# A decoder layer in split fp32: later slices of the up projection as 512-column products, and a new written order

## The chip, the cores and the metric

The kernel runs on one core of a Trainium2 chip. The time is the device time of one execution in microseconds; the median of several runs is given. The profile is of one further execution. TensorE multiplies, VectorE and ScalarE do elementwise work, GpSimd sets constants, and SyncE (SP) issues nearly all transfers.

## What is computed

One decoder layer on 256 tokens (S) of width 1024 (D), batch 1, with an adaptive norm whose shifts, scales and gates come from a conditioning vector c:

```python
mod = (c @ w_ada + b_ada)              # sh1, sc1, g1, sh2, sc2, g2
h = rmsnorm(x, norm1_g) * (1 + sc1) + sh1
z = h @ w_in                           # q, k, v, xr, gr
...                                    # attention (8 heads of 64), RG-LRU with a conv of width 4
x = x + g1 * (mix @ w_out)
h2 = rmsnorm(x, norm2_g) * (1 + sc2) + sh2
up = causal_dwconv(h2 @ w_up, ffn_conv_w, ffn_conv_b)     # width 3, 2 * 2816 columns
gate, val = split(up)
x = x + g2 * ((silu(gate) * val) @ w_down)
```

Everything is fp32 at the kernel's border.

## The kernel before

**Split products.** A weight block w is cast to a high part `wh` (`hi`, L158; L144 on ScalarE, or L150 on VectorE with a last argument 1), and the rest is `wl = w - wh` (`lo`, L172, VectorE). The activations are split the same way: for norm n and k block kt, `normed` (VectorE) makes x times scale times 1/rms, `h_hi` the high part with the shift added (ScalarE, or VectorE with argument 1), `h_lo` the rest (VectorE). The parts are two tiles `hh` and `hl` of 8 k blocks by 256 tokens. Each logical product is then three: `wh` with `hh`, `wh` with `hl`, `wl` with `hh`, summed in PSUM.

**Stages.** (1) Beginning: loads; `x_sq`, `x_sum`, `norm_s`, `norm_r`, `norm_mm` make 1/rms for norm 1; `m1_mm`, `m1_row`, `m1_col`, `m1_add` make scale and shift of the first k blocks from two loads of w_ada ("g1" 0 and 1) by a vector product, a copy of the row, a turn into a column and an add; `warm_up(n)` issues n filler products on a constant; `sp` are 18 tiny VectorE steps on the RG-LRU's decay. (2) `lin`: the input projection over 8 k blocks, with `x`, `g`, `q` as 256-column products and `k` as 512-column ones; `ada` computes further columns of mod with reductions on VectorE. (3) `v`, convolution, gates, the scan, attention. (4) `wo`: output projection. (5) norm 2: `res`, `res_sq`, `res_add`, `res_sum` (one block each), four vector products `g1_mm(6)` to `g1_mm(9)` with `g1_row`, `g1_col`, `g1_add` for its scale, `norm_s`, `norm_r`, `norm_mm`, then `normed`, `h_hi`, `h_lo` block by block. (6) The channel part: 22 slices f of 128 gate and 128 value columns. `up(f, kt)` does six products for one k block into one bank (four banks in turn). `gated_a` (ScalarE) reads the bank with the last tap's weight and the bias, `gated_d` (VectorE) adds two shifted taps, both out of PSUM; then `gated_s` (SiLU), `gated_m`, `gated_h`, `gated_l`, and `down(f, m)` with three products for each of 8 output blocks.

**Order.** Every engine works in the order in which the calls are written. From the first call to slice 3 of `up` they are written out one by one (some 640 calls); from slice 4 on a loop issues `up(f)`, the `gated` steps of f - 1 with the weight splits of f + 1 between them, and `down(f - 2)`. In the passes f = 7, 9, 11 and 13 two reductions `ada("g2", ...)` stand in it as well.

**Loads.** `order` is the list of weight loads, 1 MB each, sent on SP's queue into six buffers, the next whenever one comes free (`used`). The vector c in 128 copies (`cb`, 512 KB) is sent between them; only `ada` needs it. The split weights have three buffers.

Of the kernel before, what the change touches and what calls it, by code (L numbers as in the profile page):

```python
# [49 lines left out]
NSPLIT = 3  # L50

# [17 lines left out]
def hybrid_layer(ctx: ExitStack, tc: tile.TileContext, x_d, c_d, pk_d, bd_d, ada1_d, lin_d, v_d,  # L69
# [36 lines left out]
    order += [("g1", 2), ("g1", 3), ("wo", 0), ("g1", 4), ("g1", 5), ("wo", 1)]  # L106
# [647 lines left out]
    def gated_a(f):  # L754
        cv = get(T, ("cv", f), m4)
        for s in range(2):
            i = 2 * f + s
            nc.scalar.activation(cv[:, s, :], pair(B["up", f])[:, s, :], AF.Identity, scale=col(O_FW + 88 + i),  # L758
                                 bias=col(O_FB + i))

    def gated_d(f, s):
        cv = T["cv", f]
        i = 2 * f + s
        for j in (1, 0):
            d = 2 - j
            nc.vector.scalar_tensor_tensor(cv[:, s, d:], pair(B["up", f])[:, s, :S - d], col(O_FW + 44 * j + i),  # L766
# [33 lines left out]
    kept.enter_context(tc.manual_schedule())  # L800
    warm_up(9)
    x_sq(0)
    x_sq(1)
    consts()
    c_cols()
    x_add(0, 1)
    x_sq(2)
    x_add(0, 2)
    x_sq(3)
# [7 lines left out]
    sp_act()  # L817
    warm_up(2)
    sp(0)
    warm_up(4)  # L820
    m1_mm(0, 1, 4)
    norm_mm("n1")
    m1_row(0, 0)
    m1_row(0, 1)
    m1_col(0, 0)
    norm_c()
    m1_col(0, 1)
    m1_add(0, 0)
    normed(0, 0)
    hi("lin", 0, 0)  # L830
    m1_add(0, 1)
    sp(1)
    h_hi(0, 0, 1)
    sp(2)
    hi("lin", 0, 1)
    h_lo(0, 0)
    warm_up(2)
    lin(0, "x", 0)
    lin(0, "x", 1)
    lin(0, "g", 0)  # L840
    lin(0, "g", 1)
    m1_mm(1, 0, 7)
    lo("lin", 0, 1)
    m1_row(1, 0)
    sp(3)
    lo("lin", 0, 0)
    lin(0, "q", 1)
    m1_col(1, 0)
    lin(0, "q", 0)
    m1_mm(1, 1, 7)  # L850
    m1_row(1, 1)
    hi("lin", 1, 0)
# [707 lines left out]
```

## Time and profile before

| | |
|---|---|
| runs | 332.77 us median of 3 (332.19 to 333.26) |
| the profiled execution | 332.59 us, its span 330.8 us |
| granted TensorE clock over the span | 0.991 |
| TensorE busy | 320.2 us (97%) |
| VectorE busy | 263.0 us (79%) |
| ScalarE busy | 194.5 us (59%) |
| read from memory | 76.43 MB, 234 GB/s over the span |

The span runs from the first to the last instruction; some 1.8 us of the time lie around it. Products are pipelined: one is shown with its whole way through the array, so distances between starts tell the rate, and a busy TensorE can still stand between two instructions. The granted clock is the share of full speed that the chip gives TensorE.

### The profile page before, as it was taken

To read this page: it belongs to the slowest core of one execution; us is meant where nothing else is said; L and a number is where in the kernel's file an instruction comes from. 1 tells how busy PE (TensorE), PEld (TensorE's weight loads), DVE (VectorE), ACT (ScalarE), POOL (GpSimd) and SP (SyncE) were. 2 spreads that over 40 slices of the span, in tenths; PEclk is the share of its full clock that TensorE was granted. 3 is DMA by queue.
4 is the path that set the end of the run, shared out by engine and by line. 5 is a ranking of instruction groups with operands and counts; after the bars stand their busy time and mean duration, and the time that the engine had idled before them with its cause. 6 is when DMAs were issued, how large, how long until landed. Compare 5 with 4: busy or idle time off the path is not lost.

```text
span 330.8 us, 6467 instructions
## 1 busy us (share of the span) xinstructions
PE 320.2 (97%) x2608; PEld 302.6 (91%) x2608; DVE 263.0 (79%) x507; ACT 194.5 (59%) x328; POOL 4.6 (1%) x22
## 2 busy tenths in 40 slices
PE   7899999999999999899999999999999999999994
PEld 7789999767599996899999999999999999999994
DVE  2469999899999998968696788888888677685654
ACT  5635458999988245865566455464646464655520
POOL 5000000000000000000000000000000000000000
PEclk9999999999999999799999999999999999999998
DMA  7999999939355998836566557575849463300003
GB/s 224 337 405 408 410 408 422 411 136 385 131 162 206 345 407 316 348 129 254 167 223 248 174 214 264 206 293 183 323 146 364 135 242 133 129 0 2 3 0 127
DMA packets 18013, 77.89 MB, mean 235 GB/s; under 512 B 1600, under 2 KB 6336, under 8 KB 10944
## 3 DMA queue, kind: packets, MB, share of 16 engines
q1 hardware_dynamic: 17840, 77.34, 62.6%
q8 instruction: 20, 0.33, 0.4%
q10 hardware_dynamic: 144, 0.15, 0.2%
q14 instruction: 9, 0.07, 0.1%
HBM read 76.43 MB, written 1.05 MB: 234 GB/s over the span
## 4 chain that ended last, share of the span: by engine, by line
PE 69%; DVE 16%; ACT 6%; issue 3%; SPq 2%; DMA 2%; DVEq 0%; ACTq 0%
PE bank L65 68%; DVE wl L172 4%; DVE w L365 4%; DMA w<-in_dram 2%; DVE m L423 2%; ACT wh L144 1%; SPq L132 1%; DVE m L766 1%; PE bank L676 1%; DVE ht L381 1%; ACT p L670 1%; DVE m L794 1%; DVE m L458 1%; DVE wh L150 1%; SPq L181 1%
## 5 line engine op out<-in xcount | busy, mean ns | idle before, releaser
L172 DVE TENSOR_TENSOR wl<-w,wh 128x1024 fp32r<-128x1024 f32 x94 | 113.2, 1220 | 19.8 <-ACT wh L144 19.1
L144 ACT CAST wh<-w 128x1024 fp32r<-128x1024 f32 x90 | 92.1, 1043 | 43.6 <-PE bank L65 34.9
L65 PE MATMUL bank<-hh__1575,wh 128*128 128x256 f32 x352 | 71.6, 285 | 1.1 <-ACT hh__1575 L148 1.1
L65 PE MATMUL bank<-hl__1576,wh 128*128 128x256 f32 x352 | 71.7, 286 | 0.0
L65 PE MATMUL bank<-hh__1575,wl 128*128 128x256 f32 x352 | 71.6, 285 | 0.0
L65 PEld LDWEIGHTS bank<-hh__1575,wh 128*128 128x128 f32 x352 | 55.3, 193 | 1.3 <-ACT hh__1575 L148 1.3
L65 PEld LDWEIGHTS bank<-hl__1576,wh 128*128 128x128 f32 x352 | 55.6, 194 | 0.2 <-DVE hl__1576 L392 0.2
L65 PEld LDWEIGHTS bank<-hh__1575,wl 128*128 128x128 f32 x352 | 55.4, 194 | 0.2 <-DVE wl L172 0.2
L766 DVE SCALAR_TENSOR_TENSOR m<-bank,pk,m 128x255 f32<-128x255 f32 x88 | 40.4, 479 | 19.0 <-ACT m L758 17.4
L65 PE MATMUL bank<-pl,wh 128*128 128x256 f32 x176 | 49.9, 284 | 0.4 <-DVE pl L782 0.4
L65 PE MATMUL bank<-ph,wh 128*128 128x256 f32 x176 | 49.9, 284 | 0.0
L65 PE MATMUL bank<-ph,wl 128*128 128x256 f32 x176 | 49.8, 283 | 0.0
L65 PEld LDWEIGHTS bank<-pl,wh 128*128 128x128 f32 x176 | 33.8, 192 | 0.6 <-DVE pl L782 0.6
L65 PEld LDWEIGHTS bank<-ph,wh 128*128 128x128 f32 x176 | 33.8, 192 | 0.1
L65 PEld LDWEIGHTS bank<-ph,wl 128*128 128x128 f32 x176 | 33.8, 192 | 0.0
L758 ACT ACTIVATE m<-bank,pk 128x256 f32<-128x256 f32 x44 | 22.4, 558 | 18.9 <-PE bank L65 18.9
L365 DVE CUSTOM_DVE_ANT_0 w<-w,cb 128x1024 f32<-128x1024 f32 x22 | 26.3, 1218 | 0.0
L770 ACT ACTIVATE m<-m 128x256 f32<-128x256 f32 x22 | 9.2, 417 | 26.8 <-DVE m L766 26.8
L65 PE MATMUL bank<-hl_mix__1178,wh 128*128 128x256 f32 x64 | 18.3, 286 | 0.2 <-DVE hl_mix__1178 L505 0.2
L65 PE MATMUL bank<-hh_mix__1177,wh 128*128 128x256 f32 x64 | 18.4, 288 | 0.0
L65 PE MATMUL bank<-hh_mix__1177,wl 128*128 128x256 f32 x64 | 18.1, 283 | 0.0
L65 PE MATMUL bank<-hh__245,wh 128*128 128x256 f32 x96 | 14.8, 283 | 1.0 <-DVE lt L345 1.0
(176 smaller groups left out, 429.5 us busy)
## 6 DMA issues: line engine op xcount, KB each, us to landing
w<-in_dram SPq DMA_DIRECT2D x55, 1024.0 KB, 5.1
w<-in_dram SPq DMA_DIRECT2D x32, 512.0 KB, 10.1
xT<-in_dram SPq DMA_DIRECT2D x4, 256.0 KB, 4.5
cb<-in_dram SPq DMA_DIRECT2D x1, 512.0 KB, 9.7
out_dram<-m SPq DMA_DIRECT2D x4, 128.0 KB, 2.5
out_dram<-m SPq DMA_DIRECT2D x2, 256.0 KB, 2.8
m<-in_dram SPq DMA_DIRECT2D x1, 256.0 KB, 9.5
pk<-in_dram ACTq DMA_DIRECT2D x1, 145.0 KB, 4.0
```

The costliest lines, as they stand in the source:

```text
L65: self.nc.tensor.matmul(out, lhsT, rhs, start=left == self.n, stop=left == 1, skip_group_check=True)
L132: (q or nc.sync).dma_start(raw[key][:, c:c + n], srcs[key[0]][key[1]][:, c:c + n])
L144: nc.scalar.copy(out, in_)
L150: nc.vector.tensor_copy(out, in_)
L172: (nc.vector if e else nc.gpsimd).tensor_sub(l[:, c], raw[key][:, c], h.bitcast(F32)[:, c])
L181: nc.sync.dma_start(xT[:, 2 * i:2 * i + 2, :], x_d[:, 2 * i:2 * i + 2, :])
L365: nc.vector.tensor_tensor_reduce(v[:, a, :], v[:, a, :], cb, scale=scale, scalar=0.0, op0=ALU.mult, op1=ALU.add, accum_out=mod[:, j, kt:kt ...
L381: nc.vector.scalar_tensor_tensor(T["ht", n, kt], xT[:, kt, :], mod[:, (SC1, SC2)[n], kt:kt + 1], rep, op0=ALU.mult, op1=ALU.mult)
L423: nc.vector.scalar_tensor_tensor(xc[:, t, s:], pair(B["x", t // 2])[:, t % 2, :S - s], col(O_CW + 4 * j + t), xc[:, t, s:], op0=ALU.mult, ...
L758: nc.scalar.activation(cv[:, s, :], pair(B["up", f])[:, s, :], AF.Identity, scale=col(O_FW + 88 + i), bias=col(O_FB + i))
L766: nc.vector.scalar_tensor_tensor(cv[:, s, d:], pair(B["up", f])[:, s, :S - d], col(O_FW + 44 * j + i), cv[:, s, d:], op0=ALU.mult, op1=ALU ...
L770: nc.scalar.activation(T["cv", f][:, 2, :], T["cv", f][:, 0, :], AF.Silu)
```

## The change

- Slices 4 to 20 (`WIDE`): the two parts of h lie in one tile (k block, part, token), and `wh` streams both in one 512-column product into a bank of its own for each half of the slice, whose left side takes `wh` with `hh` and the right side `wh` with `hl`; `wl` with `hh` is a 256-column product added into the left side. A slice has two banks, and two slices share the four. `gated_a` copies the right sides out (ScalarE), adds the left sides (VectorE), and it and `gated_d` then work from that sum in SBUF. Slices 0 to 3 and 21 stay as they were.
- The loads: "g1" 4 and 5 come ahead of "wo" 0, and `cb` is sent after four weight loads instead of three.
- The written order up to slice 3 is new from the first call on; below are its beginning and norm 2. Over the part between them the operations are the same in another order, with another table call here and there. Weight casts ahead of the first product of `wo`: on ScalarE five before and eight after, on VectorE four before and two after. Behind norm 2 five casts (`up` 1, 3 and twice 4, `dn` 0) move from ScalarE to VectorE, as do three of `h_hi`, and `table(AF.Sqrt)`, `table(AF.Exp)`, `table(AF.Silu)` are asked for after the first two slices' SiLU.
- `keep_warm(n)` is a new function: n filler products into bank 3; it is called with 2 and with 3 in norm 2.

```diff
+WIDE = range(4, NF - 1)
...
-    order += [("g1", 2), ("g1", 3), ("wo", 0), ("g1", 4), ("g1", 5), ("wo", 1)]
+    order += [("g1", 2), ("g1", 3), ("g1", 4), ("g1", 5), ("wo", 0), ("wo", 1)]
...
-        if i == 2:
+        if i == 3:
             nc.sync.dma_start(cb, c_d.to_broadcast([P, D]))
...
+    def keep_warm(n):
+
+        b = get(B, "idle", lambda: bank(3, 1))
+        for _ in range(n):
+            b.reopen(1)
+            b.mm(b.t[:, 0:P], ident, ident)
...
+    def h_both(n):
+
+        return get(T, ("hx", n), lambda: big.tile([P, KT, 2, S], F32R, tag="hx", name=f"hx_{n}_"))
+
     def h_of(n):
-        return get(T, ("h", n), lambda: [big.tile([P, KT, S], F32R, tag=t, name=f"{t}_{n}_") for t in ("hh", "hl")])
+        return [h_both(n)[:, :, part, :] for part in range(2)]
...
     def up(f, kt):
+        wh, wl = spl["up", f]
+        if f in WIDE:
+
+            hx = h_both(1)
+            for s in range(2):
+                b = get(B, ("up", f, s), lambda: bank(((7, 6), (5, 2))[f % 2][s], 16))
+                w = slice(kt * 256 + s * P, kt * 256 + (s + 1) * P)
+                b.mm(pair(b), wh[:, w], hx[:, kt, :, :])
+                b.mm(b.t[:, 0:S], wl[:, w], hx[:, kt, 0, :])
+            return
         b = get(B, ("up", f), lambda: bank((7, 6, 5, 2)[f % 4], 48))
-        wh, wl = spl["up", f]
         hh, hl = h_of(1)
...
     def gated_a(f):
         cv = get(T, ("cv", f), m4)
+        if f in WIDE:
+            T["y", f] = cv[:, 2:4, :]
+            for s in range(2):
+                affine(0, T["y", f][:, s, :], B["up", f, s].t[:, S:])
+            for s in range(2):
+                nc.vector.tensor_add(T["y", f][:, s, :], T["y", f][:, s, :], B["up", f, s].t[:, 0:S])
         for s in range(2):
             i = 2 * f + s
-            nc.scalar.activation(cv[:, s, :], pair(B["up", f])[:, s, :], AF.Identity, scale=col(O_FW + 88 + i),
-                                 bias=col(O_FB + i))
+            y = T["y", f] if f in WIDE else pair(B["up", f])
+            nc.scalar.activation(cv[:, s, :], y[:, s, :], AF.Identity, scale=col(O_FW + 88 + i), bias=col(O_FB + i))
...
+        y = T["y", f] if f in WIDE else pair(B["up", f])
         for j in (1, 0):
             d = 2 - j
-            nc.vector.scalar_tensor_tensor(cv[:, s, d:], pair(B["up", f])[:, s, :S - d], col(O_FW + 44 * j + i),
+            nc.vector.scalar_tensor_tensor(cv[:, s, d:], y[:, s, :S - d], col(O_FW + 44 * j + i),
                                            cv[:, s, d:], op0=ALU.mult, op1=ALU.add)
```

The beginning, the calls in the order before (left) and after (right), `sp` steps and `c_cols` left out:

```
before                              after
warm_up(9)                          table(AF.Exp)
x_sq, x_add, consts                 warm_up(9)
table(AF.Sqrt)                      sp_act()
warm_up(12)                         x_sq, x_add, consts
x_sum, norm_s, norm_r               table(AF.Sqrt)
m1_mm(0, 0, 4)                      warm_up(9)
sp_act()                            x_sum, norm_s, norm_r
warm_up(2), warm_up(4)              m1_mm(0, 0, 4)
m1_mm(0, 1, 4)                      m1_row(0, 0)
norm_mm("n1")                       warm_up(1)
m1_row(0, 0), m1_row(0, 1)          m1_col(0, 0), m1_add(0, 0)
m1_col(0, 0)                        m1_mm(0, 1, 4)
norm_c()                            norm_mm("n1")
m1_col(0, 1)                        m1_row(0, 1)
m1_add(0, 0)                        normed(0, 0)
normed(0, 0)                        m1_col(0, 1), m1_add(0, 1)
hi("lin", 0, 0)                     hi("lin", 0, 0)
m1_add(0, 1)                        h_hi(0, 0, 1)
h_hi(0, 0, 1)                       norm_c()
hi("lin", 0, 1)                     warm_up(2)
h_lo(0, 0)                          hi("lin", 0, 1)
warm_up(2)                          table(AF.Gelu_apprx_tanh)
lin(0, "x", 0)                      lin(0, "g", 0)
```

Norm 2 in the same way, from the last product of `wo` on:

```
before                              after
wo(3, 1)                            wo(3, 6)
hi("up", 0, 0)                      res_sq(5), g1_mm(9), res(7), g1_mm(6), res(6)
res_add(5), res(7), res_sum(5)      res_add(4), res_sq(7), g1_mm(7), res_add(5)
res(6), lo("up", 0, 0), res_sq(7)   lo("up", 0, 0), res_sum(5), res_sq(6)
hi("up", 0, 1), ada_add("s2", 0)    hi("up", 1, 0), res_sum(7), hi("up", 1, 1, 1)
g1_mm(8), g1_mm(7), lo("up", 0, 1)  lo("up", 1, 1), res_sum(6)
res_sq(6), res_sum(6)               norm_s("n2"), g1_mm(8)
hi("up", 1, 0), res_sum(7)          keep_warm(2)
g1_mm(9), norm_s("n2")              g1_row(1), norm_r(), g1_col(1)
g1_row(1), norm_r(), g1_col(1)      norm_mm("n2")
lo("up", 1, 0)                      keep_warm(3)
norm_mm("n2")                       lo("up", 1, 0)
g1_add(1), normed(1, 2)             g1_add(1), normed(1, 2)
h_hi(1, 2), normed(1, 3)            h_hi(1, 2, 1), h_lo(1, 2), normed(1, 0)
h_hi(1, 3), h_lo(1, 2), h_lo(1, 3)  normed(1, 3), h_hi(1, 0), h_lo(1, 0)
up(0, 2)                            normed(1, 7), up(1, 2), up(0, 2)
```

Before, `g1_mm(6)` stands among the last third of the `wo` calls.

## Rows read from the trace of the kernel before

**Rows 1.** The page, its first part: busy time of an engine.

```profile
PE 320.2 (97%) x2608; PEld 302.6 (91%) x2608; DVE 263.0 (79%) x507; ACT 194.5 (59%) x328; POOL 4.6 (1%) x22
```

**Rows 2.** Stages: us, PE, PEld, DVE, ACT, POOL busy (count), PEclk, DMA share, GB/s.

```profile
60.00:80.00 20.00, 19.50 (x127) 14.78 (x126) 18.73 (x41) 19.38 (x36) 0.00 (x0) 1.00 0.72 296
80.00:100.00 20.00, 19.73 (x163) 14.71 (x162) 19.16 (x70) 18.29 (x52) 0.00 (x0) 1.00 0.51 182
```

**Rows 3.** The chain that ended last: start us, us, what.

```profile
14.37 0.48 DVE ht L381
15.00 0.30 DVE hh__245 L152
...
154.69 170.06 PE bank L65 x1415
```

**Rows 4.** TensorE's timeline in a later slice: start us, us, instruction.

```profile
251.14 0.40 PE L65 MATMUL bank<-hh__1575,wh 128*128 128x256 f32 x2
...
256.90 0.28 PE L65 MATMUL bank<-ph,wh 128*128 128x256 f32 x1
```

**Rows 5.** VectorE's timeline in the loop; in brackets the wait before it.

```profile
197.46 2.36 DVE L172 TENSOR_TENSOR wl<-w,wh 128x1024 fp32r<-128x1024 f32 x2 [0.77 <-ACT wh L144]
...
203.69 1.22 DVE L172 TENSOR_TENSOR wl<-w,wh 128x1024 fp32r<-128x1024 f32 x1
206.31 1.91 DVE L766 SCALAR_TENSOR_TENSOR m<-bank,pk,m 128x255 f32<-128x255 f32 x4 [1.40 <-ACT m L758]
```

**Rows 6.** TensorE's timeline, products of 512 columns in the value projection.

```profile
74.43 1.07 PE L65 MATMUL bank<-wh,hh__245 128*128 128x512 f32 x4
...
77.15 1.07 PE L65 MATMUL bank<-wh,hh__245 128*128 128x512 f32 x4
```

**Rows 7.** TensorE's timeline, 512 and 256 columns mixed in the input projection.

```profile
39.68 0.63 PE L65 MATMUL bank<-wl,hh__245 128*128 128x512 f32 x2
40.15 0.62 PE L65 MATMUL bank<-hh__245,wh 128*128 128x256 f32 x4
40.61 0.64 PE L65 MATMUL bank<-hh__245,wl 128*128 128x256 f32 x4
```

**Rows 8.** Instructions grouped by line: busy us, mean ns, idle before.

```profile
L365 DVE CUSTOM_DVE_ANT_0 w<-w,cb 128x1024 f32<-128x1024 f32 x22 | 26.3, 1218 | 0.0
L758 ACT ACTIVATE m<-bank,pk 128x256 f32<-128x256 f32 x44 | 22.4, 558 | 18.9 <-PE bank L65 18.9
...
L144 ACT COPY row<-bank 128x256 f32<-128x256 f32 x3 | 1.1, 376 | 0.8 <-PE bank L65 0.8
...
L488 DVE TENSOR_TENSOR m<-m,bank 128x256 f32<-128x256 f32 x4 | 1.4, 401 | 0.3 <-PE bank L65 0.3
```

**Rows 9.** TensorE's timeline at the start.

```profile
10.01 0.64 PE L65 MATMUL bank<-w,ccol 128*32 128x128 f32 x16
...
12.12 0.65 PE L65 MATMUL bank<-w,ccol 128*32 128x128 f32 x16
...
15.45 0.71 PE L65 MATMUL bank<-hh__245,wh 128*128 128x256 f32 x4 [0.97 <-DVE lt L345]
```

**Rows 10.** ScalarE's timeline at the start.

```profile
12.83 0.43 ACT L144 COPY m<-bank 128x128 f32<-128x128 f32 x2 [0.84 <-PE bank L65]
...
21.00 1.05 ACT L144 CAST wh<-w 128x1024 fp32r<-128x1024 f32 x1 [0.47 <-DMA w<-in_dram]
```

**Rows 11.** TensorE's timeline around norm 2.

```profile
130.95 0.61 PE L65 MATMUL bank<-sel,row 128*128 128x4 f32 x4 [0.49 <-ACT row L144]
...
133.23 0.58 PE L65 MATMUL bank<-hh__1575,wh 128*128 128x256 f32 x2 [1.11 <-ACT hh__1575 L148]
...
134.77 0.63 PE L65 MATMUL bank<-hh__1575,wh 128*128 128x256 f32 x2
...
136.90 0.42 PE L65 MATMUL bank<-hh__1575,wl 128*128 128x256 f32 x2
```

**Rows 12.** One microsecond of the table of stretches, columns as in rows 2.

```profile
134.00:135.00 1.00, 1.00 (x6) 1.00 (x7) 1.00 (x4) 0.48 (x1) 0.00 (x0) 0.50 0.96 401
```

More of the change, by code (lines that the diff above doesn't have):

```diff
@@ L800, in hybrid_layer @@
     kept.enter_context(tc.manual_schedule())
+    table(AF.Exp)
     warm_up(9)
+    sp_act()
     x_sq(0)
-    x_sq(1)
-    consts()
+    consts()
+    sp(0)
+    sp(1)
+    sp(2)
+    sp(3)
+    x_sq(1)
+    sp(4)
+    sp(5)
+    x_sq(2)
+    x_add(0, 1)
+    x_sq(3)
+    x_add(0, 2)
     c_cols()
[L806 to L809, printed above, removed]
+    table(AF.Sqrt)
     x_add(0, 3)
-    table(AF.Sqrt)
-    warm_up(12)
+    warm_up(9)
     x_sum()
@@ new lines, in hybrid_layer @@
+    ada_add("ada1", 1)
+    lin(2, "k", 1)
+    sp(13)
+    normed(0, 3)
+    h_hi(0, 3)
+    lin(2, "q", 0)
+    lin(2, "q", 2)
+    lo("lin", 3, 0)
+    lin(2, "g", 1)
+    h_lo(0, 3)
+    ada("ada1", 2, 0)
+    ada("ada1", 2, 1)
+    ada_add("ada1", 2)
+    hi("lin", 3, 1)
+    lo("lin", 3, 1)
+    lin(2, "x", 2)
+    hi("lin", 4, 0)
+    lin(2, "k", 2)
+    lin(2, "k", 0)
+    lin(2, "g", 2)
+    normed(0, 4)
+    lin(2, "q", 1)
+    lin(3, "x", 0)
+    lin(3, "x", 2)
+    lo("lin", 4, 0)
+    lin(3, "q", 0)
@@ L981, in hybrid_layer @@
-    lo("lin", 6, 0)
+    lin(4, "x", 2)
+    lin(4, "k", 0)
+    lin(4, "q", 1)
+    normed(0, 5)
+    h_hi(0, 5)
+    lo("lin", 5, 0)
+    lin(4, "k", 1)
+    h_lo(0, 5)
+    ada("ada1", 4, 0)
+    lin(4, "g", 0)
+    lin(4, "q", 0)
+    lin(4, "x", 1)
+    ada("ada1", 4, 1)
+    hi("lin", 5, 1)
+    lin(4, "g", 2)
+    lin(4, "q", 2)
+    sp(15)
+    hi("lin", 6, 0)
+    ada_add("ada1", 4)
+    normed(0, 6)
+    lin(4, "g", 1)
+    lo("lin", 5, 1)
     h_hi(0, 6)
     h_lo(0, 6)
+    hi("lin", 6, 1)
@@ L984, in hybrid_layer @@
+    lin(4, "k", 2)
+    lin(5, "g", 0)
+    table(AF.Gelu_apprx_tanh)
+    lin(5, "x", 1)
+    lo("lin", 6, 0)
+    c_more(3)
+    lin(5, "g", 2)
+    hi("lin", 7, 0)
     ada("ada1", 5, 0)
-    c_more(1)
-    hi("lin", 6, 1)
+    lin(5, "q", 1)
+    lin(5, "k", 0)
     lin(5, "x", 2)
-    table(AF.Exp)
+    lin(5, "x", 0)
+    lin(5, "q", 0)
+    lin(5, "g", 1)
+    lin(6, "x", 0)
     lin(6, "g", 0)
     ada("ada1", 5, 1)
-    table(AF.Gelu_apprx_tanh)
     ada_add("ada1", 5)
-    sp(11)
+    lin(6, "g", 1)
@@ L1175, in hybrid_layer @@
-    hi("wo", 2, 1, 1)
-    s_exp(7)
     pv(3)
@@ L1320, in hybrid_layer @@
     g1_col(1)
+    norm_mm("n2")
+    keep_warm(3)
     lo("up", 1, 0)
-    norm_mm("n2")
     g1_add(1)
     normed(1, 2)
-    h_hi(1, 2)
+    h_hi(1, 2, 1)
+    ada_add("s2", 0)
+    h_lo(1, 2)
+    normed(1, 0)
     normed(1, 3)
+    h_hi(1, 0)
+    h_lo(1, 0)
+    normed(1, 7)
+    up(1, 2)
+    up(0, 2)
     h_hi(1, 3)
-    h_lo(1, 2)
+    normed(1, 1)
     h_lo(1, 3)
-    up(0, 2)
-    table(AF.Sqrt)
-    normed(1, 7)
-    normed(1, 1)
+    hi("up", 0, 1)
+    up(0, 0)
+    normed(1, 4)
     h_hi(1, 7)
-    up(1, 2)
@@ new lines, in hybrid_layer @@
+    gated_d(1, 0)
+    up(2, 3)
+    up(2, 5)
+    up(2, 7)
+    gated_d(0, 1)
+    gated_d(1, 1)
+    gated_s(0)
+    gated_m(0)
+    gated_s(1)
+    table(AF.Sqrt)
+    hi("dn", 0, 1, 1)
+    gated_m(1)
+    up(3, 6)
+    up(3, 4)
+    gated_h(0)
+    hi("dn", 0, 0)
+    up(3, 7)
+    table(AF.Exp)
+    gated_l(0)
+    lo("dn", 0, 0)
+    up(2, 6)
+    up(2, 2)
+    hi("up", 4, 0, 1)
+    up(3, 5)
+    up(3, 0)
+    down(0, 3)
+    gated_h(1)
+    table(AF.Silu)
+    up(3, 2)
+    gated_l(1)
```

803 lines of the change are left out of this document (356 added, 447 removed).

## The prediction

> **What bounds the kernel now.** I read the page first: TensorE is busy for 320.2 of 330.8 us [rows 1]. A busy TensorE is not yet the bound, so the second view is the table by stage: from 60 to 100 us VectorE is busy for 37.9 and ScalarE for 37.7 of 40 us, and the transfers, at 296 and 182 GB/s, are far from their pace in other stages [rows 2]. The third view, the chain that ended last, gives the split. Its start runs over VectorE (the first normed block at 14.37, its high part at 15.00), and its last long link is one piece of TensorE alone, 1415 products in 170.06 us, 120.2 ns each [rows 3]. So three different things set the time: a chain of small steps up to the first large product at 15.45 us, VectorE and ScalarE from there to the output projection, and TensorE's own rate from 154.69 us to the end.
>
> That rate is the same in the timeline of TensorE: one slice of `up` starts at 251.14, the next `down` at 256.90, so 48 products take 5.76 us, 120 ns each [rows 4]. A slice with its `down` is 72 products or 8.64 us, two slices 17.28 us.
>
> VectorE's timeline in this loop shows how far it is ahead. In one pair of slices it waits twice, 0.77 us for a weight cast and 1.40 us for ScalarE's bias pass, which itself waits for the products; it works 17.28 - 0.77 - 1.40 = 15.1 us [rows 5]. The low half of the next slice's weights ends at 203.69 + 1.22 = 204.9, and its slice starts at 251.14 - 5 x 8.64 = 207.94, so the first half has at least 3 us to spare [rows 4, 5].
>
> **The wide product.** In 17 slices each group (one k block, one 128 column half) has three products of 256 columns now, 3 x 120 = 360 ns. The change makes it one of 512 and one of 256. The trace has 512-column products in this type: in the long run of `v`, 12 of them take 77.15 - 74.43 = 2.72 us, 226.7 ns each [rows 6]. A group then takes 227 + 120 = 347 ns and saves 13 ns; 17 x 8 x 2 = 272 groups save 3.5 us. Bounds from the mixed stretch, where 512 and 256 alternate as they will here: two of 512 take 40.15 - 39.68 = 0.47 us, 235 ns each, and the four of 256 behind them 40.61 - 40.15 = 0.46 us, 115 ns each [rows 7]. 235 + 120 = 355 saves 5 ns or 1.4 us; 227 + 115 = 342 saves 18 ns or 4.9 us. I take the long run, since the loop is as long and as regular: 3.5 us.
>
> The Trainium skill ("TensorE: Matmul & The Clock Gate", section "Back-to-back issue gap") puts the gap at columns over 2.4 GHz plus 2.5 ns. By it merging two products saves 2.5 ns, 0.7 us over the kernel as an estimate, and the sum below would be 329.5. The trace does not agree: 120 ns at 256 and 227 ns at 512 columns differ by 107 ns, the same as the page's, but stand some 13 ns above the streaming time, and the measurement decides [rows 4, 6].
>
> What it costs: both halves of a slice now lie in a pair of banks as two sums that must be added. Per slice two copies on ScalarE (a 128x256 copy out of PSUM takes 0.38 us) and two adds on VectorE (an operation with one PSUM operand takes 0.40 us), ahead of the two bias passes (0.56 us each now) [rows 8]. VectorE per pair of slices: 15.1 + 4 x 0.40 = 16.7 us, while TensorE's pair shrinks to 2 x (16 x 0.347 + 24 x 0.12) = 16.9 us. This is close. It is hidden as long as the handshake (copy, add, bias pass, taps) adds less than the spare time: the second add runs beside the first bias pass, so I estimate s = 0.2 us of wait per slice. The pair read here carries two reductions of 1.2 us for g2 [rows 8], as the four pairs at slices 7 to 13 do; these fall behind by 4 x (0.4 - 0.2) = 0.8 us, under the 3 us to spare, and the 4.5 other pairs have 0.2 + 2.4 = 2.6 us of room each. Nothing on the path. The banks hold two slices instead of four, but the adds free them, and the pair is wanted again only two slices later; for the narrow last slice, which takes one bank of slice 20's pair, the cover is the 24 products of `down` between them, 2.9 us, against 0.8 us of copies and 0.8 us of adds. If that cover is gone it costs up to 1 us, once.
>
> **The beginning.** Today the two vector products of g1 stand at 10.01 and 12.12 with 12 filler products between, both of their row copies start only after the second, at 12.83, and the first large product at 15.45 [rows 9, 10]. In the new order the first row is copied, turned and added between the two products, with one filler. From 12.83 to the normed block at 14.37 it is 1.54 us for both copies, turns and adds [rows 3, 10]; half of it is 0.77. The second product then starts at 10.01 + 0.64 + 0.77 + 0.25 = 11.7, 0.4 us sooner, and its own copy, turn and add take 0.77 us less: 1.2 us, the first product at 14.25. Upper bound: the second product ends at 12.77, and 0.48 + 0.30 us for normed block and high part must follow, 15.45 - 13.55 = 1.9 us. Lower bound: zero, if weights set the pace behind it. ScalarE waits for the data of `lin` 1 at 21.00 [rows 10]; the change sends the 512 KB of `cb` after `lin` 1 instead of before, and `cb` is wanted only by the first reduction, so this wait moves forward as well. The early Exp table, the logs of the decay (`sp`) and one more table load lie on ScalarE and VectorE while both wait for data, at nothing: ScalarE has only the two copies and a cast to do around them [rows 10]. I take 1.2 us.
>
> **Norm 2.** From 134 to 135 us the granted clock is 0.50, that is 1.2 instead of 2.4 GHz [rows 12]. TensorE had stood still before, 0.49 us for the row copy and 1.11 us for the first high part, and then 10 products from 134.77 to 136.90 take 213 ns each instead of 120, the 6 before them 1.54 us instead of 0.72 [rows 11]. Against 120 ns each that is 0.93 + 0.82 = 1.75 us, some 0.15 of it waits for low parts. A filler takes about 0.25 us (six of them between 10.01 + 0.64 and 12.12 [rows 9]); the five of `keep_warm`, 1.25 us, fit into the 1.6 us of standing. A fourth vector product moves behind `wo` and leaves the same time ahead of it. So 1.6 us if the clock stays up. It is not all kept: at full rate the first two slices ask for a block of h every 12 x 0.12 = 1.44 us, VectorE has 0.48 us for the normed block, about as much for the low part and 0.30 for the high part of every second one [rows 3], some 1.1, and weight halves of 1.2 us between, so I give back 0.4: 1.2 us. Bounds: a loss of 0.5, if the clock falls all the same and a filler stands in the way, and a gain of 1.75. In the first four slices behind it five weight casts move to VectorE (1.05 us at most each) and three table loads are asked for in a row; 240 products, 28.8 us at 120 ns, lie beside them, so at nothing; uncovered they would show as a wait for a low part ahead of slice 4.
>
> **The middle.** The order from 57 to 100 us is rewritten with the same operations. Two places differ in load: three more weight casts (1.05 us each [rows 10]) lie on ScalarE ahead of the first product of `wo`, eight instead of five, two fewer on VectorE; and two g1 transfers go ahead of a `wo` one on SP's queue, whose pace leaves room for that. With 2.3 us of ScalarE's 40 idle there [rows 2], the casts cost between nothing (attention's tail has `wo`'s products as cover) and 3.1 us; a better order could win as much. Taken as 0.
>
> **The sum.** Against the profiled execution, 330.8 us of span and 332.6 us in all: 332.6 - 3.5 - 1.2 - 1.2 = 326.7 us. It stands 0.2 us under the median of the runs, so no shift.
>
> **Rivals.** (a) The wide product saves little, 5 ns a group, as in the mixed stretch: 326.7 + 2.1 = 328.8. For it: the alternation there is the one here; against: those stretches are short. The page's gap, named above, belongs to this case. (b) The casts on ScalarE come onto the path: 326.7 + 3.1 = 329.8. (c) The middle wins as much as (b) loses, 323.6. For both: two engines without room take each wait of the order in full; against: the work is the same. (d) Slower: VectorE becomes the bound of the loop. With copies and bias passes fully serial with the adds, s = 2 x 0.38 + 2 x 0.5 = 1.8 us a slice; the four heavy pairs then lose 2 x 1.8 - 0.2 = 3.4 us each, the 4.5 others 3.6 - 2.6 = 1.0 each, less 3 us to spare: 15 us, 342. It turns the sign from s of about 1.35 us on (4 x 2.5 + 4.5 x 0.1 - 3 = 7.5). For it: VectorE has 0.2 us per pair left. Against: TensorE's part is done long before, so ScalarE's copies can run ahead.
>
> **Chances.** Forecast 0.48, (a) 0.17, (b) 0.13, (c) 0.11, (d) 0.11. The likeliest one's own range is 324 to 329.5, from the bounds of the wide product (plus 2.1, minus 1.4) and of the other two. Over 331.6 lie most of (d) and a part of (b) and (a); 0.3% or 1 us is about what a measurement here can tell. Faster 0.82, same 0.08, slower 0.10. The range leaves out most of (d) and little of (c): 321.5 to 331.8.
>
> **What would show it.** In the changed profile: a slice of `up` of 5.55 us in place of 5.76; no TensorE wait for VectorE from slice 5 on, VectorE near 19 of 20 us; the first large product near 14.2; a granted clock of 1.00 through norm 2. The forecast is wrong if TensorE's gaps in the loop name VectorE, or if the first product of `up`, at 133.23 today, comes no sooner in spite of the earlier start.

## The result and the profile after

The changed kernel takes 329.12 us (median of 18 runs, 327.55 to 336.97), the kernel before in the same rounds 332.59 us (18 runs, 330.92 to 333.33). The ratio is 0.990, interval 0.988 to 0.992: 3.5 us faster. The ratios here and below leave out runs more than 1.5% above the fastest of their kernel, two of the 18 here; medians and ranges hold all runs. Forecast were 326.7 us, in a range of 321.5 to 331.8.

The profiled execution took 327.9 us with a span of 326.1 us, 4.7 us under the span before. Its busy line on the page:

```profile
PE 315.8 (97%) x2330; PEld 286.6 (88%) x2330; DVE 280.9 (86%) x551; ACT 202.1 (62%) x354; POOL 4.6 (1%) x22
```

Against [rows 1] TensorE has 278 products fewer and still the same share of the span, so it stays the bound; VectorE has taken 18 us more. The chain that ended last (start us, us, what), the answer to [rows 3]:

```profile
12.78 0.48 DVE ht L389
...
13.86 4.64 PE bank L66 x60
...
19.16 36.04 PE bank L66 x258
...
132.90 187.20 PE bank L66 x1300
```

It begins over VectorE as before. Through the input projection it now runs over TensorE (36.04 us from 19.16 on). The last long link of TensorE begins with the first product of `up`, at 132.90 instead of 154.69 us: there is no wait left between norm 2 and the end.

Five marks on TensorE's timeline and one on ScalarE's (the first exponential of the softmax) cut both spans into stages; a mark is the start of an instruction, in us from the span's start:

| stage | before | after | difference |
|---|---|---|---|
| to the first large product | 15.45 | 13.86 | -1.6 |
| from there to the first exponential | 68.52 | 67.06 | -1.5 |
| from there to the first product of `wo` | 16.25 | 19.19 | +2.9 |
| `wo` and norm 2, to the first product of `up` | 33.01 | 32.79 | -0.2 |
| from there to slice 4 | 31.51 | 29.10 | -2.4 |
| slice 4 to the end of slice 21's `up` | 152.64 | 150.72 | -1.9 |
| rest | 13.4 | 13.4 | 0.0 |
| span | 330.8 | 326.1 | -4.7 |

The forecast for the wide product was -3.5 and for the middle 0; the middle, from the first large product to the first of `wo`, is +1.5 in sum. The clock matters in this table: before, the profile shows it at 0.50 at 134 us [rows 12] and at 0.57 over 133 to 137, after, at 1.00 in every stage up to 320 us. That differs from run to run. Of the 18 runs after, 4 have a mean granted clock of 0.998 or more and spans of 325.8 to 326.1 us, 9 have 0.993 to 0.995 and 326.7 to 327.7, the other 5 less. Of the runs before, those at 0.997 or more have spans of 328.9 to 329.9. So the change is worth some 3 us at full clock, and the medians hold beside it what the clock does in each kernel.

**Start, loop and norm 2 on TensorE.** Its timeline at the start, for [rows 9]:

```profile
9.73 0.64 PE L66 MATMUL bank<-w,ccol 128*32 128x128 f32 x16
...
11.45 0.64 PE L66 MATMUL bank<-w,ccol 128*32 128x128 f32 x16 [0.31 <-DVE mod L621]
...
13.86 2.39 PE L66 MATMUL bank<-hx__243,wh 128*128 128x256 f32 x18 [0.44 <-DVE lt L359]
```

One wide slice and the `down` behind it, for [rows 4]:

```profile
187.59 0.40 PE L66 MATMUL bank<-hx__1571,wh 128*128 128x512 f32 x1
187.82 0.28 PE L66 MATMUL bank<-hx__1571,wl 128*128 128x256 f32 x1
187.94 0.39 PE L66 MATMUL bank<-hx__1571,wh 128*128 128x512 f32 x1
...
193.23 0.28 PE L66 MATMUL bank<-ph,wh 128*128 128x256 f32 x1
```

16 groups take 193.23 - 187.59 = 5.64 us, 352.5 ns each; it was 5.76, and 5.55 was forecast. Over the loop the 512-column product is followed after 236 ns and the 256-column one after 117 ns on average.

Norm 2, for [rows 11], and one microsecond of the table of stretches, for [rows 12]:

```profile
132.90 0.94 PE L66 MATMUL bank<-hx__1571,wh 128*128 128x256 f32 x4 [0.56 <-DVE mod L383]
133.67 0.40 PE L66 MATMUL bank<-hx__1571,wl 128*128 128x256 f32 x2
133.91 0.64 PE L66 MATMUL bank<-hx__1571,wh 128*128 128x256 f32 x4
```

```profile
134.00:135.00 1.00, 1.00 (x10) 1.00 (x9) 0.81 (x3) 1.00 (x3) 0.00 (x0) 1.00 0.99 418
```

The clock is 1.00, and the six products that took 1.54 us take 133.91 - 132.90 = 1.01.

**VectorE in the loop**, for [rows 5]:

```profile
185.81 0.74 DVE L782 TENSOR_TENSOR m<-m,bank 128x256 f32<-128x256 f32 x2
186.89 1.91 DVE L794 SCALAR_TENSOR_TENSOR m<-m,pk 128x255 f32<-128x255 f32 x4 [0.34 <-ACT m L786]
```

The two adds and a wait of 0.34 us for the bias pass are the whole handshake; 0.2 us was the estimate. No TensorE instruction between 160 and 320 us waits for VectorE.

**The middle**, two stages for [rows 2]; then the stretch from the first exponential to the first product of `wo`, before (first line) and after (second); then the weight casts on ScalarE between the softmax's exponentials:

```profile
60.00:80.00 20.00, 19.68 (x150) 13.60 (x150) 18.70 (x38) 18.98 (x34) 0.00 (x0) 1.00 0.76 306
80.00:100.00 20.00, 18.42 (x130) 14.70 (x130) 18.81 (x71) 18.80 (x51) 0.00 (x0) 1.00 0.55 206
```

```profile
83.97:100.22 16.25, 15.98 (x132) 12.51 (x131) 15.48 (x60) 15.28 (x49) 0.00 (x0) 1.00 0.51 172
80.92:100.11 19.19, 17.61 (x128) 14.08 (x127) 18.03 (x65) 18.91 (x51) 0.00 (x0) 1.00 0.53 196
```

```profile
82.00 1.03 ACT L145 CAST wh<-w 128x1024 fp32r<-128x1024 f32 x1
...
84.01 1.04 ACT L145 CAST wh<-w 128x1024 fp32r<-128x1024 f32 x1
...
91.16 1.04 ACT L145 CAST wh<-w 128x1024 fp32r<-128x1024 f32 x1
...
93.89 1.06 ACT L145 CAST wh<-w 128x1024 fp32r<-128x1024 f32 x1
```

Before, ScalarE casts no weight between 84 and 99 us; its exponentials stand close together there, and three casts lie ahead of them, at 78.05, 79.47 and 80.89. Now the first exponential comes 3.05 us sooner, 1.6 of them from the start, and four casts lie among the exponentials: the stretch to the first product of `wo` has 3.6 us more work on ScalarE and is 2.9 us longer. So the +1.5 of the middle is a gain of 1.5 ahead of the exponentials and a loss of 2.9 in them. TensorE is thinner in this stage: 18.42 instead of 19.73 of 20 us. The chain that ended last runs over these casts and exponentials from 80.92 to 97.5 us.

### The profile page after: what moved, and what is told of

The parts are those of the page before. It is cut to its first block, busy times and chain, and to the rows that moved or that the text cites. A ratio compares the mean times of both kernels' runs of the same rounds, so it can differ in the third digit from the quotient of the medians.

```text
span 326.1 us, 5996 instructions
## 1 busy us (share of the span) xinstructions
PE 315.8 (97%) x2330; PEld 286.6 (88%) x2330; DVE 280.9 (86%) x551; ACT 202.1 (62%) x354; POOL 4.6 (1%) x22
## 4 chain that ended last, share of the span: by engine, by line
PE 81%; ACT 10%; DVE 6%; issue 1%; POOL 0%; DVEq 0%; ACTq 0%; POOLq 0%
PE bank L66 81%; ACT p L682 3%; DVE wl L173 2%; ACT wh L145 1%; ACT pt L145 1%; DVE m L822 1%; ACT m L454 1%; ACT m L457 0%; ACT m L149 0%; ACT m L145 0%; ACT L461 0%; ACT L454 0%; ACT L223 0%; DVE ssk L554 0%; DVE m L464 0%
## 5 line engine op out<-in xcount | busy, mean ns | idle before, releaser
L66 PE MATMUL bank<-hx__1571,wh 128*128 128x512 f32 (+1 forms) x432 | 122.8, 356 | 0.6 <-DVE mod L383 0.6
L145 ACT CAST wh<-w 128x1024 fp32r<-128x1024 f32 x87 | 89.8, 1044 | 33.9 <-PE bank L66 22.1
L66 PE MATMUL bank<-hx__1571,wl 128*128 128x256 f32 x352 | 92.5, 281 | 0.0
L66 PEld LDWEIGHTS bank<-hx__1571,wh 128*128 128x128 f32 x432 | 73.2, 189 | 12.7 <-PE bank L66 0.7
L66 PEld LDWEIGHTS bank<-hx__1571,wl 128*128 128x128 f32 x352 | 63.9, 190 | 0.0
L794 DVE SCALAR_TENSOR_TENSOR m<-m,pk 128x255 f32<-128x255 f32 x68 | 31.4, 482 | 7.0 <-ACT m L786 5.8
L786 ACT ACTIVATE m<-m,pk 128x256 f32<-128x256 f32 x34 | 18.6, 595 | 22.2 <-DVE m L782 22.2
L66 PE MATMUL bank<-hx__243,wh 128*128 128x256 f32 x192 | 27.2, 284 | 0.5 <-DVE lt L359 0.4
L66 PEld LDWEIGHTS bank<-hx__243,wh 128*128 128x128 f32 x192 | 25.2, 190 | 2.3 <-ACT rrep L145 0.6
L66 PE MATMUL bank<-hx_mix__1164,wh 128*128 128x256 f32 x128 | 23.6, 285 | 0.2 <-DVE hx_mix__1164 L517 0.2
L66 PEld LDWEIGHTS bank<-hx_mix__1164,wh 128*128 128x128 f32 x128 | 20.0, 192 | 0.5 <-DVE hx_mix__1164 L517 0.4
L66 PE MATMUL bank<-wh,hx__243 128*128 128x512 f32 x64 | 18.2, 401 | 0.0
L66 PE MATMUL bank<-hx_mix__1164,wl 128*128 128x256 f32 x64 | 18.2, 284 | 0.0
```

What stands on the lines that cost most here:

```text
L66: self.nc.tensor.matmul(out, lhsT, rhs, start=left == self.n, stop=left == 1, skip_group_check=True)
L145: nc.scalar.copy(out, in_)
L786: nc.scalar.activation(cv[:, s, :], y[:, s, :], AF.Identity, scale=col(O_FW + 88 + i), bias=col(O_FB + i))
L794: nc.vector.scalar_tensor_tensor(cv[:, s, d:], y[:, s, :S - d], col(O_FW + 44 * j + i), cv[:, s, d:], op0=ALU.mult, op1=ALU.add)
```

## The experiments

Twelve kernels ran, each beside the kernel before on the same chip. "Spans at full clock" are those of runs with a mean granted clock of 0.996 or more, with their number.

| kernel | median us (range), runs | ratio to before, interval | spans at full clock |
|---|---|---|---|
| changed | 329.12 (327.55 to 336.97), 18 | 0.990, 0.988 to 0.992 | 325.8 to 326.1 (4) |
| e1 wide only | 330.64 (329.01 to 331.80), 12 | 0.995, 0.993 to 0.998 | 327.2 to 327.6 (3) |
| e2 order only | 331.14 (329.81 to 338.82), 12 | 0.997, 0.994 to 1.000 | 328.0 to 328.1 (3) |
| e3 no fillers in norm 2 | 329.33 (328.54 to 330.81), 6 | 0.991, 0.988 to 0.994 | none |
| e4 grouped | 326.92 (326.11 to 333.53), 6 | 0.985, 0.980 to 0.989 | 324.3 to 324.7 (3) |
| e5 beginning only | 331.93 (330.77 to 333.77), 10 | 1.000, 0.998 to 1.002 | none |
| e6 fillers only | 331.21 (330.83 to 333.08), 10 | 0.998, 0.995 to 1.001 | 329.1 to 329.7 (9) |
| e7 casts late | 330.00 (328.70 to 334.01), 10 | 0.995, 0.991 to 0.998 | 326.9 to 327.8 (4) |
| e8 fillers in attention | 328.69 (328.40 to 329.96), 7 | 0.991, 0.988 to 0.994 | 326.6 to 327.0 (6) |
| e9 combined | 327.19 (326.79 to 327.57), 6 | 0.984, 0.981 to 0.986 | 325.0 to 325.8 (6) |
| e10 pairs | 327.59 (326.90 to 329.13), 5 | 0.984, 0.980 to 0.988 | 325.1 to 325.8 (3) |
| e11 four more adds | 342.26, one run | - | none (340.5 at 0.981) |
| e12 other bank | 328.17 (327.69 to 329.80), 4 | 0.987, 0.982 to 0.992 | 325.9 to 326.6 (3) |

**The change in halves.** e1 gives the kernel before the wide slices alone, with the order and the loads of before; e2 has the new order and loads alone.

```diff
-WIDE = range(4, NF - 1)
+WIDE = range(0)            # e2
```

> The kernel before with the wide product alone, in the written order of before. Theory: the loop gets shorter by what the product pairs give at the rates of the changed kernel's trace, 236 + 117 = 353 instead of 360 ns in 272 groups, 1.9 us, and norm 2 stays as it was, with the clock at half for 3.4 us behind it: 330.7 us. Rival (VectorE): the added copies and adds make VectorE late and the gain is lost or turned, 332.6 or more. Rival (width): the product is worth the 3.5 us of the prediction and something else in the new order ate it, 329.1.

> The changed kernel with no wide slice (WIDE empty): order, beginning, loads and fillers alone. Theory: the time from the first product of up to the loop keeps its 2.4 us and the start of norm 2 its 0.3: 2.7 us less than before in executions in which the granted clock stays up, 329.9, and some executions slower by 1.7 us for each 3.4 us at half clock. Rival: the order is worth nothing by itself, 332.6, and all of the gain is the product's.

e1 is 1.8 us shorter at full clock, its loop takes 150.72 us, 1.9 less than before, and its wide slice 5.65 us: the product is worth half of what I forecast, the rest of the forecast isn't hidden somewhere else. e2's loop is 152.64 us, as before to the last digit; at full clock it is 1.1 us shorter, and its interval touches 1.

**Where the beginning went.** e5 is the kernel before with the changed kernel's first calls and `cb` after four loads; the order behind is the old one.

```diff
-        if i == 2:
+        if i == 3:
...
+    m1_row(0, 0)
+    warm_up(1)
+    m1_col(0, 0)
+    m1_add(0, 0)
     m1_mm(0, 1, 4)             # and on as in the table of the change, to h_lo(0, 0)
```

> The kernel before with the changed kernel's calls up to the second large product (and cb after four loads); everything behind them in the order of before. Theory: the first large product comes at 13.9 us as in the changed kernel, 1.6 us sooner, and in the order of before nothing eats it until the scores: the first product of wo 1.2 us or more sooner, 331.0. Rival: VectorE and the loads set the pace of the input projection and the gain is gone by the convolution: 332.4 and the first product of wo at 100.2 as now.

Its profile has the first large product at 14.26, the first of `wo` at 99.23 (before 100.22) and the first of `up` at 132.25 us (before 133.23): in this profile 1.0 us of the 1.2 stays up to norm 2. I expected 1.2 or more. Marks at the start differ by several tenths from profile to profile of the same calls. With the old beginning the first large product comes at 15.37 to 15.76 us (before, e1, e6); with the new one at 13.79 to 14.69 in ten profiles, on average 14.1, and at 14.96 in e10, whose clock was at 0.50 from 12 to 16 us. So the beginning wins 1.4 us on average. e9 and e12, below, have e5's calls up to `wo`; in e5, e9 and e12 its first product comes at 99.23, 99.40 and 100.28, in before, e1 and e6 at 100.12 to 100.52: 0.7 us of the gain are left there on average, between none and most of it in a single profile.

The median doesn't show it, ratio 1.000 with 0.2% either way, since the clocks differ: none of e5's ten runs has 0.996 or more, ten of the 28 runs of before beside it have. At like mean clocks (0.986 to 0.995) nine of its ten spans lie 0.5 to 2.0 us under the median span of before. The tenth is at 0.981, where before has no run. The new order of the loads was not run by itself.

With the changed order the first product of `wo` comes at 100.11: by then the 1.6 us won at the start, and 1.5 more won ahead of the exponentials, are lost. The split is the same in every profile: from the first large product to the first exponential it takes 66.6 to 67.2 us in the new order (seven profiles) and 68.5 to 69.3 in the old one (six; the seventh, e10, started with its clock at half). From the first to the last exponential's end it takes 13.97 or 13.98 us in all seven of the old order, and 16.9 to 19.5 in the six of the new order that have all four casts (16.92 in the changed kernel's; the others have a fall of the clock there or, in e8, more fillers).

e7 takes two of the `wo` casts that the new order puts among the exponentials, the one right behind them, and the splits that need these, and places all of them later (on the grouped loop of e4, below):

```diff
-    hi("wo", 2, 0)            # behind s_exp(4)
-    hi("wo", 2, 1)            # behind p_T(5)
-    hi("wo", 1, 1)            # behind p_copy(6, 0)
+    hi("wo", 2, 0)            # behind p_copy(6, 0)
...
+    hi("wo", 2, 1)            # behind wo(0, 3)
...
+    hi("wo", 1, 1)            # behind o_m(1)
```

> The grouped kernel with the casts of wo 2 (both halves) and of wo 1 (second half) moved from between the exponentials of the scores to behind them, and the products of wo 0 first. Theory (rival b of the prediction): ScalarE is without idle time from 84 to 98 us and two of the four casts there lie between exponentials, so the first product of wo comes about 1.5 us sooner than in the changed kernel, where it starts at 100.11, and the time in executions with the clock up falls from 326.1 to 324.8. Rival: transposes and products of the attention set the pace, or the casts are only late elsewhere: no change.

The first product of `wo` comes 0.5 us sooner (99.58), but the last 1.9 us later than in the changed kernel (126.49 against 124.59), for the products now wait for their casts. Against e4 it is 2.2 to 3.5 us worse at full clock. From the first to the last exponential it takes 16.65 us, only 0.27 less, though two casts of 0.94 us are gone: ScalarE now waits 0.73 and 0.69 us there for transposes on TensorE, where the kernel before has one such wait, of 0.69. So the expected 1.5 did not come, and the rival that transposes and products set the pace was right for these two. The two early casts, at 82.00 and 84.01, stayed where they are; what they cost by themselves no run shows. These casts can't simply be moved.

**Norm 2 and the clock.** e3 takes both `keep_warm` calls out of the changed kernel; e6 puts them alone into the kernel before, around its `norm_s("n2")` and `norm_mm("n2")`.

```diff
     norm_s("n2")
+    keep_warm(2)               # e6; e3 removes both from the changed kernel
     g1_row(1)
...
     norm_mm("n2")
+    keep_warm(3)
```

> The changed kernel without the five fillers of keep_warm; nothing else is left out. Theory: the granted clock falls to half behind norm 2 in this profile as in that of before, 16 products at 213 instead of 120 ns, about 1.5 us more than the changed kernel, 330.6. Rival: the fillers don't matter, since the new order has less idle time there: same time as the changed kernel and a clock of 1.00 in norm 2.

> The kernel before with the five fillers of keep_warm at the same two places of norm 2, nothing else. Theory of the prediction: the granted clock stays at 1.00 behind norm 2, where the profiles of before and of the kernel with the wide product alone show 0.50; 1.6 us less, 330.8. Rival: five short products are too few to change the clock's course there; 332.4, clock 0.50 for 3 us from 133 us.

In e6 the clock holds, in a row of TensorE's timeline and one of the table of stretches:

```profile
133.53 0.50 PE L65 MATMUL bank<-hh__1581,wh 128*128 128x256 f32 x2 [0.45 <-ACT hh__1581 L148]
134.05 0.50 PE L65 MATMUL bank<-hl__1582,wh 128*128 128x256 f32 x2
134.39 0.40 PE L65 MATMUL bank<-hh__1581,wl 128*128 128x256 f32 x2
```

```profile
134.00:135.00 1.00, 0.98 (x9) 0.95 (x9) 1.00 (x3) 0.18 (x1) 0.00 (x0) 1.00 0.95 393
```

From the first product of `up` to slice 4 it takes 30.12 us, 1.4 less than before; 9 of 10 runs have a clock of 0.997 or more, where 15 of the 69 runs of before beside these experiments have. Its median is 1.1 us lower, with an interval that still touches 1. That is the mechanism of the prediction, alone. In the changed kernel it fails to show: e3 without fillers has the same time as with them, 0.991 against 0.990. Its profile says why:

```profile
92.00:96.00 4.00, 4.00 (x24) 3.35 (x24) 2.61 (x19) 3.19 (x9) 0.00 (x0) 0.57 0.74 262
133.00:137.00 4.00, 2.97 (x23) 2.84 (x24) 3.76 (x11) 2.17 (x5) 0.00 (x0) 1.00 1.02 430
```

Norm 2 runs at full clock without a filler, and from the first product of `up` to slice 4 it takes 29.09 us, as with them (29.10), against 30.1 in the old order with fillers (e6, e9). So the changed kernel's 29.1 is the new order's; its fillers add nothing. The clock is at 0.57 from 92 to 96 us, in the attention, as in e2's profile. Just before, from 88 to 92 us, TensorE is busy for 3.11 of 4 us in e3 and 3.13 in the changed kernel, 4.00 in the kernel before. So the new order thins TensorE out between the exponentials, and in these profiles the clock falls there. Whether it falls differs from run to run: the changed kernel's own profile has none.

e8 fills that stretch: 16 single filler products into bank 1 among the calls of the attention (on e4's loop).

```diff
+    def mid_warm(n):
+        b = get(B, "mid", lambda: bank(1, 1))
+        for _ in range(n):
+            b.reopen(1)
+            b.mm(b.t[:, 0:P], ident, ident)
```

> The grouped kernel with a filler product behind each transpose and each product of the probabilities with v, sixteen in all, where the clock fell in three profiles (92 us on). Theory: the falls come from the thin TensorE work in the attention, the fillers stop them: every execution within 0.6 us and near 326.2 to 326.8, no clock under 0.997. Rival: the fillers hold up the chain from exponential to transpose more than they give, or the clock falls all the same: a third of the executions 1 to 7 us over the fastest, as in the grouped kernel.

The clock stays up in 6 of 7 runs, at 0.996 or more, but the first product of `wo` comes at 102.29 us, 2.2 later than in the changed kernel, and the spans are 2.3 us over e4's at full clock. The fillers cost more than they give: its median is 1.8 us above e4's.

**Why the wide product saves 7 ns a group, not 13.** e4 keeps the sums and reorders each wide slice's products:

```diff
+        for part in range(2):        # wh with both parts, then wl
+            for kt in range(KT):
+                for s in range(2):
...
+                    if part == 0:
+                        bs[s].mm(pair(bs[s]), wh[:, w], hx[:, kt, :, :])
+                    else:
+                        bs[s].mm(bs[s].t[:, 0:S], wl[:, w], hx[:, kt, 0, :])
```

> The changed kernel with the products of a wide slice in another order: first all 16 of 512 columns, then all 16 of 256. Theory (alternation): a 512-column product takes 236 ns because a 256-column one follows it; in a run it takes 227 as in the value projection, a slice 16 x 0.227 + 16 x 0.12 = 5.55 us instead of 5.64, 17 slices 1.6 us less, 327.5. Rival (loop): 235 ns belong to the loop, where VectorE, ScalarE and the transfers use the memory at the same time: no change, 329.1.

The same slice on its TensorE timeline:

```profile
185.90 3.82 PE L66 MATMUL bank<-hx__1571,wh 128*128 128x512 f32 x16
189.56 2.08 PE L66 MATMUL bank<-hx__1571,wl 128*128 128x256 f32 x16
191.47 0.28 PE L66 MATMUL bank<-ph,wh 128*128 128x256 f32 x1
```

16 products of 512 columns in 3.66 us are 229 ns each, 16 of 256 in 1.91 us 119: 348 ns a group, the forecast's 347. The slice takes 5.57 us, the loop 149.35, 1.4 less than changed. It is the fastest at full clock, though its profile has the clock at half from 92 to 109 us and its runs spread to 333.5.

e9 puts together what held: the kernel before with e5's beginning, e6's fillers and e4's grouped slices. e10 is e9 with the k blocks outside (512, 512, 256, 256 for each); e12 is e9 with widths alternating as in the changed kernel, but consecutive products always in different banks.

```diff
-        for part in range(2):
-            for kt in range(KT):
+        for kt in range(KT):            # e10
+            for part in range(2):
...
+        steps = [(1, 0, 0)]             # e12: (half, part, k block)
+        for kt in range(KT):
+            steps += [(0, 0, kt), (1, 1, kt)]
+        for kt in range(1, KT):
+            steps += [(0, 1, kt - 1), (1, 0, kt)]
+        steps.append((0, 1, KT - 1))
```

> The parts that held up, put together: the order of before from the third large product on, the changed kernel's beginning, keep_warm at its two places in the order of before, and the grouped wide product. Theory: the parts add up where the clock stays up, before's span of 329.1 less 1.0 (beginning) and 3.5 (grouped product) and nothing for the fillers, 324.6 or 326.4 us of time, and most executions are there, since the attention keeps the order in which the clock has not fallen. Rival: the falls in the attention come with any kernel that reaches it sooner, and the median is no better than the grouped kernel's 326.9 with its spread of 7 us.

> The combined kernel with the products of a wide slice in pairs: for each k block two of 512 columns, then two of 256. Theory (alternation): a 512-column product behind a 256-column one or ahead of one pays; half of the changes of width are left, a slice between 5.57 and 5.64 us, about 5.60, and 17 slices 0.6 us more than the combined kernel. Rival: what counts is only that a 512-column product stands behind another 512-column one somewhere, 5.57; or the bank that changes from product to product is what costs, 5.64.

> The kernel is the combined one (the order of before, the new beginning, the fillers in norm 2, the fifth-slice-on loop grouped), but each wide slice now alternates 512-column and 256-column products, as the changed kernel does, with the difference that consecutive products never write the same PSUM bank. Theory (two products in a row into one bank cost TensorE some 6 ns each time, the alternation of widths costs nothing): a wide slice takes 5.57 us, the loop from its first product to the last slice's end 149.2 us, the time is 327.2 us, as the combined kernel. Rival (the alternation of widths itself lengthens the 512-column product from 227 to 236 ns): a slice takes 5.64 us, the loop 150.6 us, the time is 328.5 us.

e9 has the steadiest runs: 327.19 us, spread 0.8 us, all six at a clock of 0.997 or more. 326.4 was expected: its spans are 0.4 to 1.2 us over the sum of the parts. The order does not hold the clock up by itself: of the nine runs of e10 and e12, which have e9's calls up to the loop, three are at 0.991 or less. e10's loop takes 149.47 us against e9's 149.35: half the changes of width were expected to cost half the loss, and cost nothing. e12's loop takes 149.85 us, and its slices fall into two kinds, on its TensorE timeline:

```profile
171.92 0.62 PE L66 MATMUL bank<-hx__1573,wh 128*128 128x512 f32 x2
...
177.48 0.28 PE L66 MATMUL bank<-ph,wh 128*128 128x256 f32 x1
...
180.35 0.63 PE L66 MATMUL bank<-hx__1573,wh 128*128 128x512 f32 x2
...
185.99 0.28 PE L66 MATMUL bank<-ph,wh 128*128 128x256 f32 x1
```

The odd slices (banks 5 and 2) take 5.56 us as when grouped, the even ones (banks 7 and 6) 5.64, with the end of the second at 185.99. In the changed kernel both kinds take 5.64 or 5.65. So the alternation of widths alone isn't the cost, and two products running into one bank aren't all of it: before, all six products of a k block went to one bank at 120 ns. The order of the products in the slice decides, by 1.4 us in all; by which rule is open.

**How near VectorE is to the bound.** e11 is the changed kernel with four adds more, into an unused tile, behind each wide slice's two.

```diff
+            for s in (0, 1, 0, 1):
+                nc.vector.tensor_add(idle, T["y", f][:, s, :], T["y", f][:, s, :])
```

> The changed kernel with four more adds of 128x256 on VectorE in each wide slice, into a tile that nobody reads: 1.7 us a slice, 3.4 a pair. Theory: VectorE works 18.3 of 20 us in the loop now, so a pair has 1.4 us of room; the four heavy pairs fall behind by 2.0 us each, less 3 us to spare, 5 us more span and TensorE waits that name VectorE; the light pairs have room for all of it. Rival (d of the prediction): the room is not usable, because the handshake between the two engines takes it, and each of the 8.5 pairs loses 2 us or more: 14 us.

```profile
180.00:200.00 20.00, 20.00 (x130) 18.14 (x130) 19.34 (x36) 10.59 (x18) 0.00 (x0) 1.00 0.55 209
200.00:220.00 20.00, 19.39 (x125) 17.39 (x125) 19.33 (x36) 10.60 (x18) 0.00 (x0) 1.00 0.59 218
```

```profile
PEld bank L66 <- DVE wl L173: 4.7, 6, 1.1
...
PE bank L66 <- DVE wl L173: 2.9, 4, 0.8
PE bank L66 <- DVE m L783: 2.3, 1, 2.3
```

(Stages as in [rows 2], then the table of waits from 160 to 320 us: waiter, what it waits for, us in all, times, longest.) Four adds take 201.06 to 202.77, 1.71 us a slice or 29 us in all; the loop grew from 150.7 to 164.2 us. So 15.6 us, 0.9 a slice, went into room that VectorE had, and 13.5 came out. VectorE works 19.3 of 20 us from 180 us on; TensorE still has no gap up to 200 us, while VectorE uses up its lead, and the first slice that takes longer starts at 205.52. The 13.5 us do not fall evenly: the pairs of slices from 4 and 6 lose nothing, those from 8, 10, 12 and 14 lose 0.8, 2.8, 4.2 and 1.3, those from 16 and 18 0.3 in sum, and the last two slices 4.1, of which 2.3 are the narrow slice's wait for slice 20's adds (the last row). A part of it is the clock, 0.91 from 240 to 260 us. So my expectation was right in that the loss gathers around the heavy pairs, and far too low in size, 5 us. The rival's 14 is the measured sum by luck: it wanted 2 us or more in every pair. It is one run.

## Why the prediction was right or wrong

Right in sign and range, 2.4 us too low in time: a gain of 3.5 us where 5.9 were forecast. The time landed within 0.3 us of rival (a), 328.8. Its price for the wide product came true; that the sum did is partly luck, since the middle (+1.5), norm 2 (1.4 more than forecast) and the clock's falls (1.2 from the profiled execution to the median) were off as well and nearly cancel.

- **Bound and loop: right.** TensorE's rate sets the loop; VectorE stands at 18.3 to 18.7 us of 20 in the later slices and nothing waits for it. Rival (d) did not come, but e11 shows it about 0.9 us of VectorE's work a slice away. By the prediction's own sums the sign would have turned at a wait s of about 1.2 us already, where 4 x 2.2 - 3 = 5.8 us are lost, not at 1.35; measured was 0.34.
- **The wide product: the mis-sized term**, -3.5 forecast, -1.9 measured in the loop of both e1 and the changed kernel. Step that failed: "I take the long run, since the loop is as long and as regular". The long run of one width gives 229 + 119 in the grouped loop, so the figure was good; the changed kernel alternates, and the rows that showed the alternation, 235 for the 512-column product [rows 7], were the nearer ones. Measured: 236 + 117 = 353, rival (a)'s 355 within 2 ns. (a)'s reason holds in part only: e10 keeps half of the changes of width at no cost, and half of e12's slices alternate at no cost. The gap that the Trainium skill states ("TensorE: Matmul & The Clock Gate", section "Back-to-back issue gap") for a product by itself gave 0.7 us for the merge; no run agrees, for e1's loop saves 1.9 us and e4's 3.3.
- **The beginning: right at its place, mostly gone further on.** The first large product came 1.6 us sooner in the profile and 1.4 on average (1.2 forecast); the old order keeps 0.7 of it up to `wo` on average. In the changed kernel 0.1 is left there. The 12 products that the forecast counts between the two vector products are six fillers, two rows each, as its later sum has them.
- **The middle: "taken as 0" was wrong by 1.5 us**, and in both directions: 1.5 won ahead of the exponentials, for a reason that no run shows, and 2.9 lost in them, nearly rival (b)'s 3.1. That the loss lies with ScalarE is shown by its stretch: it works without a pause from the first exponential to the last, with four casts that the order before does not have there. That casts alone are the cause is not shown: two of them moved away gave back 0.3 us of it (e7), and transposes set the pace instead. The cover named in the prediction, `wo`'s products, lies behind the exponentials, too late for these casts.
- **Norm 2: right in the mechanism, half of the size, and not by the fillers.** -2.6 from the first `wo` product to slice 4 in the two profiles, over the forecast's upper bound of 1.75; forecast -1.2. The clock mechanism is confirmed by e6 (-1.4, in the order before). The other 1.0 is the new order of the first slices, 29.1 us up to slice 4 where the old order takes 30.1 at full clock: the 0.4 that the forecast gave back for VectorE's pace was the term of the wrong sign. In the changed kernel the fillers are not needed for the clock (e3). The `wo` stage is 1.1 us shorter and norm 2 0.9 longer up to the first product of `up`: one vector product, 1.0 us long, moved from the one into the other, as forecast at no gain. What the forecast didn't see is that the clock would fall in another stretch: in 14 of 18 runs of the changed kernel it was below 0.998. The forecast's "a granted clock of 1.00 through norm 2" came true, and the median still pays for a fall.
- **The signs that were named**: slice 5.64, not 5.55; no TensorE wait for VectorE, right; first large product 13.86 for 14.2; clock 1.00 in norm 2, right; first product of `up` at 132.90 for 133.23, only 0.3 sooner. That last one is met by a hair, and only where the clock stayed up (134.03 and 134.38 in e3 and e2, where it fell); it did point to the middle.

By parts, in the profiles: -1.6 + 1.5 - 2.6 - 1.9 = -4.6 against the span's -4.7; forecast -1.2 + 0 - 1.2 - 3.5 = -5.9, from a profile whose clock had fallen.

## What to carry to other kernels

Price a merged instruction by rows in the order in which it will stand, and if a long run of one kind is cheaper, write the loop as long runs: here the same products grouped by width gave another 1.4 us, and in pairs 1.25. A gain at the start is worth what is left of it at the next place where two engines are full, so follow it to there by marks, in more than one profile, before counting it. A stage that comes out even may hide a gain and a loss: cut it once more where the engines' work changes. A clock that falls in one stretch of the order before may fall in another of the new one; compare runs with their clocks, and prefer the order whose runs stay close together (e9) to one that is faster only in its best runs (e4).

## What the runs showed of the hardware

- A 512-column product costs 227 to 229 ns and a 256-column one 119 to 120 in runs of their own, 236 and 117 alternating in the changed kernel's order, 233 and 115 in pairs: the sum for a group, 353 or 348 ns, depends on the order of products and banks, not on the widths alone; by which rule is open.
- The same program has its clock fall in some runs and not in others: spans of one kernel (e4) from 324.3 to 331.7 us at mean clocks of 1.00 to 0.973.
- With four adds more (e11), VectorE worked 19.1 to 19.4 of each 20 us from 180 to 320 us. TensorE had no gap from 180 to 200 us, and stood for 0.6 to 2.4 of each 20 us from 200 to 280.
